# Eight groups of block products in a gated MLP's up projection instead of seven, with three reorderings beside it

## The chip, the cores and the metric

The kernel runs on one core of a Trainium2 chip. The metric is the device time of one execution in microseconds; three executions of the kernel before took 675.86, 676.35 and 676.62 us. The five engines of the core are named PE (TensorE, matrix products; PEld is its loading of weights), DVE (VectorE), ACT (ScalarE), POOL (GpSimd) and SP (SyncE, which issues most of the DMAs). They run side by side; each takes its instructions in the order in which the program issued them, and waits on semaphores where an operand is not ready or a buffer is not free.

## The reference

One decoder layer for a sequence of T = 512 tokens and D = 1024 features, all in float32. Its first part (a conditioned norm, an input projection, two kinds of attention heads, an output projection) is not touched by the change. The second part is:

```python
h2 = rmsnorm(x, norm2_g) * (1.0 + sc2) + sh2          # (512, 1024)
u = causal_dwconv(h2 @ w_up, conv_w, conv_b)          # w_up (1024, 2*2816); 3 taps along the tokens
a, v = jnp.split(u, 2, axis=-1)                       # (512, 2816) each
x = x + gt2 * ((jax.nn.silu(a) * v) @ w_down)         # w_down (2816, 1024)
```

`sc2`, `sh2` and `gt2` come from a small conditioning vector: `mod = silu(c) @ w_ada + b_ada`, cut in six.

## The kernel before, in words

**Products.** A float32 operand is split into a high part, rounded to the type that PE multiplies at full rate, and the low rest. `split` (lines 149 to 151) is an ACT cast for the high part and a DVE subtraction for the low part. `mm3` (lines 153 to 156) then issues three products: high times high, high times low and low times high. 512 or 256 columns stream through PE per product.

**Units and stages.** The 2816 features are 22 blocks of 128. Block j and block j + 11 form unit j, j = 0 to 10 (NU = 11). Each block needs two products with h2, one for a and one for v, so a unit has four. In *Up*, the first phase, a plain **stage** makes one of the four: `up_mm` issues 8 x 3 products of 512 columns into a PSUM bank `u`; `post_taps` takes it through the three convolution taps (`taps`: one ACT activation and two DVE operations, lines 1774 to 1776); `post_gate` applies silu on ACT and, once a and v are there, multiplies them on POOL (`gate`). HEAD lists the blocks that go through stages first, BODY those that go last. NH = 8 is the number of head stages, nst the number of all stages.

**Block products.** The units in XS go through `x_group` instead. There the a products of a unit's two blocks are made as one 2 x 2 block product (two halves of the tokens, two halves of the features, two blocks of weights) by the scheme with seven half products in place of eight. So a group has seven `x_mm` of 12 products with 256 columns (PSUM tile `uf`, with regions X, Y, Z, R) and two full v products (PSUM tile `V`, printed as `u`; 24 products of 512 columns each). The operands are sums: those of h2 are made once (`SX`), those of the weights per group, one group ahead, by `prepare_sums`, `prepare_plain`, `prepare_rest` and `prepare_other` on DVE and ACT: splits `b` (plain), `t12` and `x4` (sums), `c` (plain), `v1` and `v2`. What remains of a group after its last product (the add of Y, the taps of V[1] and of uf[0], and the gates) is put in `held` as three functions and run inside the next group, or in the first stage after the last group.

**The order** of all this is the order of the program text; the engines take it as it stands. In every quarter of a group and in every stage, `beside` advances a tick. At given ticks `weight_sums` issues DMAs that sum blocks of w_down in HBM for the second phase (some on SP, the accumulating ones on POOL), and `put_by` stores the finished products of a unit (`PB`, into `later`) in HBM. XT is the tick of the first stage after the groups; from the second of these stages on, at every other tick, `put_by` splits one of the first EARLY units' other products (`PA`) by `a_split`.

**The last gate, gt2,** is summed beside the groups: `last_add` scales a fetched piece of w_ada on ACT, adds it on POOL into the buffer `gt2`, and fetches the next one on SP; sixteen pieces in all, the first eight for the left half. Each half is then split (`last_split`: `rhi`, `rlo`), summed over the partitions and spread to all of them by two PE products (`last_spread`, line 1527), and copied back on ACT (`last_out`).

**Down,** the second phase, takes 22 blocks u. Blocks 0 to 10 use the `PA` products of units 0 to 10, blocks 11 to 21 the `PB` products. `dn_load` fetches weights on SP three blocks ahead, `dn_split` splits those of the next block (and the unit's `PA`, where it was not split early), `dn_mm` issues the products. PRE = 4 of the `PB` products come back from HBM early: `back` at block u - EARLY + 1 and `a_split` at block u - EARLY, for u counted from EARLY. Line 2124 stores the last `PB` products in block 1; SP waits there for POOL's gates.

Of the kernel before, what the change touches and what calls it, by code (L numbers as in the profile page):

```python
# [50 lines left out]
EPOS = 1  # L51
VLAG = 1
ADL = 1
EARLY = 4
PRE = 4
NU = NFF // 2
XS = (2, 3, 4, 5, 6, 7, 8)
HEAD = (0, 11, 1, 12)
BODY = (9, 20, 10, 21)
PAIRS = tuple(range(NU))  # L60
ADAS = (3, 4, 2)
ADW = 1024
# [47 lines left out]
def hybrid_layer_kernel(ctx: ExitStack, tc: tile.TileContext, d: dict, out: bass.AP, dbg=None):  # L110
# [21 lines left out]
    def PS(s="ps"):  # L132
        return psum.tile([P, 512], F32, tag="b", name=nm(s))

    def TMP(shape, dt=F32, tag="tmp"):
        n = 1
        for a in shape[1:]:
            n *= a
        if n > 256:
            return tp.tile(shape, dt, tag="t2", name=nm(tag), bufs=8)  # L140
        return tp.tile(shape, dt, tag="t1", name=nm(tag), bufs=4)
# [4 lines left out]
    def f32(ap):  # L146
        return ap.bitcast(F32)

    def split(hi, lo, src, eng=None):
        sc.copy(hi, src)  # L150
        (eng or ve).tensor_tensor(lo, src, f32(hi), ALU.subtract)  # L151

    def mm3(o, ah, al, bh, bl, start, stop):
        pe.matmul(o, ah, bh, start=start, stop=False, skip_group_check=True)  # L154
        pe.matmul(o, ah, bl, start=False, stop=False, skip_group_check=True)  # L155
        pe.matmul(o, al, bh, start=False, stop=stop, skip_group_check=True)  # L156
# [45 lines left out]
    def up_load(f):  # L202
        return load(f"up{f}", [2, KT, P], *[((slice(None), h), wu_view[:, :, h * FF + f * P:h * FF + (f + 1) * P])
                                            for h in range(2)])

    def x_load(j, h):
        return load(f"u{'xv'[h]}{j}", [2, KT, P],
                    *[((slice(None), r), wu_view[:, :, h * FF + f * P:h * FF + (f + 1) * P])
                      for r, f in enumerate((j, j + NU))])

    x_loads = [x_load(j, h) for j in XS for h in range(2)]
    loads += [*[up_load(f) for f in HEAD[:-1]], x_loads[0], up_load(HEAD[-1])]
# [3 lines left out]
    last_x = len(loads)  # L216
    loads += [up_load(f) for f in BODY]
    issued = []
# [14 lines left out]
    def take(name):  # L233

        i = taken[0]
        assert loads[i][0] == name, (loads[i][0], name)
        n = max(i + 2, min(i + 3, last_x)) if i >= first_x else i + 2
        while len(issued) < min(n, len(loads)):
            issue()
        taken[0] += 1  # L240
        return issued[i]
# [1252 lines left out]
    def last_fetch(s):  # L1494
        if last_at[0] < 2 * KT:
            q, k = divmod(last_at[0], KT)
            last_at[0] += 1
            r = TMP([P, 512], tag="aw")
            sp.dma_start(r, ada_view[:, k, s * D + q * 512:s * D + q * 512 + 512])
            last_raw.append((r, q, k))  # L1500
# [6 lines left out]
    def last_add(s, res):  # L1507
        r, q, k = last_raw.pop(0)
        acc = res[:, q * 512:(q + 1) * 512]
        sc.activation(r, r, AF.Copy, scale=cs[:, k:k + 1])  # L1510
        gp.tensor_tensor(acc, acc, r, ALU.add)  # L1511
        last_fetch(s)
# [3 lines left out]
    def last_split(res, q):  # L1516
        assert all(raw[1] > q for raw in last_raw)
        hi, lo = (TMP([P, 512], F32R, tag=t) for t in ("rhi", "rlo"))
        split(hi, lo, res[:, q * 512:(q + 1) * 512])
        last_parts.extend((hi, lo))  # L1520
# [8 lines left out]
    def last_out(res, q):  # L1529
        sc.copy(res[:, q * 512:(q + 1) * 512], last_ps.pop())  # L1530
# [227 lines left out]

    NF = HEAD + BODY

# [52 lines left out]
    def put_by(now):  # L1813
        for j in sorted(full_at, key=full_at.get):
            if now >= full_at[j] + 4:
                del full_at[j]
                sp.dma_start(later[j], PB.pop(j)[:, 0:3])
                if place[j] < EARLY:
                    unsplit.append(j)
# [68 lines left out]
    gt2 = wp.tile([P, D], F32, tag="xin", name="gt2", bufs=1)  # L1888
    lo_half, hi_half, full = slice(0, 256), slice(256, 512), slice(0, 512)
    nst = 2 * len(NF)  # L1890
    NH = 2 * len(HEAD)
    XT = NH + 4 * len(XS)
    for i in range(NT):
# [44 lines left out]
    def h_block(r, q):  # L1938
        sl = slice(256 * r, 256 * r + 256)
        return [[h2T[2 * q + k // 2][e][:, k % 2, sl] for k in range(4)] for e in range(2)]  # L1940

    def x_mm(o, w, rhs, start=True):
        for k in range(4):
            mm3(o, w[0][:, k], w[1][:, k], rhs[0][k], rhs[1][k], start and k == 0, k == 3)

    def half(w, b):
        return w[0][:, b], w[1][:, b]
# [6 lines left out]
    def prepare_sums(n):  # L1954
        raw = take(f"ux{XS[n]}")
        b11, b21, b12, b22 = (raw[:, r, k:k + 4] for r in range(2) for k in (0, 4))
        t = G([2, 4, P], s="t12")
        ve.tensor_tensor(t[:, 0], b11, b12, ALU.add)
        ve.tensor_tensor(b12, b12, b22, ALU.add)
        ve.tensor_tensor(t[:, 1], b12, b11, ALU.add)  # L1960
        prep[n] = {"raw": raw, "t": t}
# [14 lines left out]
    def prepare_other(n):  # L1976
        p = prep[n]
        p["other"] = take(f"uv{XS[n]}")
        v, t = ((KT, P), "v1"), ((2, 4, P), "t12")
# [9 lines left out]
    def x_group(n):  # L1989
        j, p = XS[n], prep[n]  # L1990
        more = n + 1 < len(XS)
        ops = {q: [[z[:, k] for k in range(4)] for z in SX[q]] for q in SX}
        h11, h12, h22 = h_block(0, 0), h_block(0, 1), h_block(1, 1)
        uf = PS("uf"), PS("uf")
        X, Y, Z, R = uf[0][:, 256:512], uf[0][:, 0:256], uf[1][:, 0:256], uf[1][:, 256:512]
        V = PS("u"), PS("u")
        m1, n5, u2 = (TMP([P, 256], tag=z) for z in ("m1", "n5", "u2"))
        beside()
        x_mm(X, half(p["b"], 0), h11)
        x_mm(Y, half(p["b"], 1), h12, False)  # L2000
        held.pop(0)()
        split(*p["t12"], p.pop("t"))
        sc.copy(m1, X)
        v_mm(V[0], p["v1"], range(4))
        held.pop(0)()
        last_add(5, gt2)
        beside()
        x_mm(X, half(p["t12"], 1), ops[2], False)
        x_mm(Z, half(p["t12"], 0), ops[1])
        sc.copy(u2, X)  # L2010
        sc.copy(n5, Z)
        v, t = ((KT, P), "v2"), ((4, P), "x4")
        for shape, name in ((v, t) if n % 2 or not more else (t, v)):
            p[name] = room(shape)
        split(*p["v2"], p.pop("other")[:, 1])
        held.pop(0)()
        v_mm(V[0], p["v1"], range(4, KT))
        if more:
            prepare_sums(n + 1)
        beside()  # L2020
        x_mm(X, half(p["c"], 0), ops[3], False)
        x_mm(Z, half(p["c"], 1), ops[4], False)
        taps(V[0], 1, j)
        split(*p["x4"], p.pop("t4"))
        ve.tensor_tensor(Z, Z, u2, ALU.subtract)
        ve.tensor_tensor(R, n5, X, ALU.subtract)  # L2026
        if more:
            prepare_plain(n + 1)
        else:
            last_add(5, gt2)  # L2030
        v_mm(V[1], p["v2"], range(4))
        taps(uf[1], 0, j + NU)
        last_add(5, gt2)
        beside()
        v_mm(V[1], p["v2"], range(4, KT))
        if more:
            prepare_rest(n + 1)
        else:
            last_add(5, gt2)
        x_mm(X, p["x4"], h22, False)  # L2040
        if more:
            prepare_other(n + 1)
        else:
            piece(True)
        del prep[n]

        def first():
            ve.tensor_tensor(Y, Y, m1, ALU.add)
            taps(V[1], 1, j + NU)

        def second():
            gate(0, j + NU)
            taps(uf[0], 0, j)

        def third():
            gate(0, j)
            gate(1, j)
            gate(1, j + NU)

        held.extend((first, second, third))  # L2060
# [30 lines left out]
    for st in range(NH, nst):  # L2091
        beside()
        if st == nst - 3:
            dn_load(0)
        elif st == nst - 1:
            dn_load(1)
        if st in (NH + 2, NH + 4):
            last_spread()
        up_mm(st, full)
        if held:  # L2100
            for f in held:
                f()
            held.clear()
        elif st > NH + 1:
            if st > NH + 2:
                post_gate(st - 3)
            post_taps(st - 2)
        if st in (NH + 1, NH + 3):
            last_split(gt2, st == NH + 3)
        if st in (NH + 2, NH + 4):  # L2110
            last_out(gt2, st == NH + 4)
    dn_split(0)
    post_gate(nst - 3)
    post_taps(nst - 2)
# [14 lines left out]
    for u in range(NU - 1):  # L2129
        ahead_of(u)  # L2130
        if u == 0:
            post_gate(nst - 2)
            post_gate(nst - 1)
        if 0 <= u - EARLY + 1 < PRE:
            back(PAIRS[u - EARLY + 1])
        if 0 <= u - EARLY < PRE:
            a_split(u - EARLY + NU, PB.pop(PAIRS[u - EARLY]))
        for m in TERMS[0]:
# [83 lines left out]
    t = TMP([P, T])[:, 0:256]  # L2222
# [36 lines left out]
```

## Time and profile before

| | |
|---|---|
| median of three executions | 676.35 us (675.86 to 676.62) |
| the profiled execution, whole | 675.84 us |
| its span, first to last instruction | 674.0 us |
| busy share of the span: PE, DVE, ACT, POOL | 98%, 81%, 57%, 26% |
| granted PE clock | 0.998 of full speed |
| first group of block products begins | 368.16 us after the span's start |
| seventh group ends | 516.42 |
| Down begins | 562.26 |

The profile is one execution, recorded by the hardware. Times in it count from the first instruction; between its span and the execution's time lie 1.84 us. A row of a timeline gives the start, the duration, the engine, the line of the kernel, the operation, the tiles written and read (without their numbers), shape and count; in brackets the engine's idle time before it and what ended that. A line can be that of a helper: L150 and L151 are the two halves of every `split`, L154 to L156 the three products of `mm3`, so the tiles tell which one it is. Products overlap in PE, so the distance from one start to the next is what a product costs, not its duration.

### The profile page before, as it was taken

The page shows a single profiled execution, that of the slowest core. Times are in us where ns is not written, and L with a number is a line of the kernel's source. Part 1 is how long each engine was busy: PE and PEld are TensorE (multiplying, and loading weights), DVE is VectorE, ACT ScalarE, POOL GpSimd, SP SyncE. Part 2 cuts the span into 40 slices and gives each one's busy share as a digit, 9 for nine tenths or more (in the row PEclk, how much of TensorE's full clock was granted, in tenths as well). Part 3 has the DMA queues.
Part 4 walks back from the last instruction along what each step waited for, and adds up shares of the span by engine and source line. Part 5 has one row for each costly group of instructions (what it writes and reads, how often), then busy time and mean ns, then how long its engine had stood idle before and what let it go on. Part 6 is the DMA issues. An engine that isn't in the chain of part 4 may idle for free.

```text
span 674.0 us, 11718 instructions
## 1 busy us (share of the span) xinstructions
PE 661.5 (98%) x4400; PEld 558.2 (83%) x4400; DVE 547.5 (81%) x1038; ACT 382.7 (57%) x713; POOL 177.5 (26%) x172
## 2 busy tenths in 40 slices
PE   8999999999999999999999999999999999999996
PEld 4778898788988888888988898898988788888885
DVE  5788988979899879688779678988888758785997
ACT  5755447756687678245555455554655556664451
POOL 1006111000010100100365455666556645000000
PEclk9999999999999999999999999999999999999999
DMA  9936264576122416144748799999997765966662
GB/s 329 411 153 205 95 197 133 183 240 220 44 85 78 143 32 230 55 130 153 233 138 226 228 221 289 242 291 274 265 266 186 219 217 162 361 219 248 219 280 94
DMA packets 101885, 134.67 MB, mean 200 GB/s; under 512 B 6507, under 2 KB 67780, under 8 KB 101829
## 3 DMA queue, kind: packets, MB, share of 16 engines
q1 hardware_dynamic: 96885, 121.28, 53.5%
q0 software_dynamic: 4512, 11.54, 10.1%
q10 hardware_dynamic: 432, 1.12, 0.5%
q8 instruction: 34, 0.56, 0.3%
q14 instruction: 22, 0.18, 0.1%
HBM read 125.39 MB, written 31.60 MB: 233 GB/s over the span
## 4 chain that ended last, share of the span: by engine, by line
PE 82%; DVE 10%; ACT 5%; issue 1%; DMA 1%; ACTq 0%; DVEq 0%
PE u L154 8%; PE u L155 8%; PE u L156 8%; PE dn L154 5%; PE dn L156 5%; PE dn L155 5%; PE uf L156 4%; PE uf L155 3%; PE uf L154 3%; PE accq L680 3%; PE oh L154 2%; PE oh L156 2%; PE oh L155 2%; PE oT L1149 2%; PE F L1120 2%; PE pT L154 2%
## 5 line engine op out<-in xcount | busy, mean ns | idle before, releaser
L151 DVE TENSOR_TENSOR wlo<-raw,whi 128x1024 fp32r<-128x1024 f32 (+1 forms) x52 | 66.3, 1277 | 43.3 <-ACT whi L150 43.2
L154 PE MATMUL u<-h2h,whi 128*128 128x512 f32 (+1 forms) x240 | 90.4, 377 | 0.0
L155 PE MATMUL u<-h2l,whi 128*128 128x512 f32 (+1 forms) x240 | 90.2, 376 | 0.0
L156 PE MATMUL u<-h2h,wlo 128*128 128x512 f32 (+1 forms) x240 | 90.0, 375 | 0.0
L150 ACT CAST whi<-raw 128x1024 fp32r<-128x1024 f32 (+1 forms) x52 | 53.0, 1020 | 32.5 <-PE u L155 25.7
L156 PEld LDWEIGHTS u<-h2h,wlo 128*128 128x128 f32 x240 | 45.2, 188 | 8.3
L154 PEld LDWEIGHTS u<-h2h,whi 128*128 128x128 f32 x240 | 45.3, 189 | 7.5
L155 PEld LDWEIGHTS u<-h2l,whi 128*128 128x128 f32 x240 | 45.3, 189 | 7.4
L150 ACT CAST whi<-wd 128x1024 fp32r<-128x1024 f32 x20 | 21.1, 1055 | 39.8 <-PE dn L156 39.8
L372 POOL TENSOR_TENSOR hrs<-hrs,mhalf 128x4 f32<-128x4 f32 (+2 forms) x16 | 18.6, 1173 | 90.7 <-DVE hrs L371 88.6
L1087 ACT ACTIVATE pt<-pt,mx 128x128 f32<-128x128 f32 (+3 forms) x64 | 35.9, 564 | 9.1 <-DVE mx L1071 8.1
L154 PE MATMUL pT<-hT,whi 128*128 128x512 f32 x96 | 38.3, 399 | 0.0
L151 DVE TENSOR_TENSOR wlo<-wd,whi 128x1024 fp32r<-128x1024 f32 x20 | 24.9, 1247 | 16.1 <-ACT whi L150 16.1
L156 PE MATMUL pT<-hT,wlo 128*128 128x512 f32 x96 | 37.5, 391 | 0.0
L155 PE MATMUL pT<-hT,whi 128*128 128x512 f32 x96 | 37.5, 391 | 0.0
L155 PE MATMUL dn<-wlo,as 128*128 128x512 f32 x88 | 34.4, 390 | 0.1
L154 PE MATMUL dn<-whi,as 128*128 128x512 f32 x88 | 34.3, 389 | 0.0
L156 PE MATMUL dn<-whi,as 128*128 128x512 f32 x88 | 34.2, 389 | 0.0
L1511 POOL TENSOR_TENSOR gt<-gt,aw 128x512 f32<-128x512 f32 x16 | 23.0, 1441 | 41.1 <-ACT aw L1510 41.0
L1127 ACT COPY pT<-F 128x512 f32<-128x512 f32 (+2 forms) x52 | 25.8, 499 | 13.2 <-PE F L1120 13.2
L1071 DVE CUSTOM_DVE_ANT_0 pt<-S,cmask 128x128 f32<-128x128 f32 (+3 forms) x64 | 29.7, 485 | 2.2 <-PE S L1067 2.0
L1774 ACT ACTIVATE y<-uf,cv 128x512 f32<-128x512 f32 x14 | 10.9, 776 | 30.2 <-DVE uf L2026 28.2
(409 smaller groups left out, 2040.7 us busy)
## 6 DMA issues: line engine op xcount, KB each, us to landing
raw<-in_w_up SPq DMA_DIRECT2D x44, 512.0 KB, 6.3
aw<-in_w_ada SPq DMA_DIRECT2D x24, 512.0 KB, 4.0
ada<-in_ada_first SPq DMA_DIRECT2D x16, 512.0 KB, 8.0
raw<-in_w_in SPq DMA_DIRECT2D x7, 1024.0 KB, 4.9
wt<-in_w_down POOLq DMA_DIRECT2D x11, 512.0 KB, 8.1
wd<-in_w_down SPq DMA_DIRECT2D x11, 512.0 KB, 5.1
wt<-in_w_down SPq DMA_DIRECT2D x10, 512.0 KB, 6.2
wt<-in_w_down POOLq DMA_DIRECT2D x5, 1024.0 KB, 10.0
```

The costliest lines, as they stand in the source:

```text
L150: sc.copy(hi, src)
L151: (eng or ve).tensor_tensor(lo, src, f32(hi), ALU.subtract)
L154: pe.matmul(o, ah, bh, start=start, stop=False, skip_group_check=True)
L155: pe.matmul(o, ah, bl, start=False, stop=False, skip_group_check=True)
L156: pe.matmul(o, al, bh, start=False, stop=stop, skip_group_check=True)
L372: gp.tensor_tensor(o, o, mhalf[:, 0:n], ALU.pow)
L680: pe.matmul(accq[i], h[:, e, i * P:(i + 1) * P], w[:, f], start=(k + e + f == 0), stop=(e == 1 and k == KT - 1), skip_group_check=True)
L1071: ve.tensor_tensor_reduce(pt[:, e * W:(e + 1) * W], ps[:, e * W:(e + 1) * W], cmask[:, 512 - W:512], -1.0, 1e30, ALU.add, ALU.min, mx[:, e ...
L1087: sc.activation(pt[:, sl], pt[:, sl], AF.Exp, bias=mx[:, e:e + 1], scale=-1.0, accum_out=su[:, h % 2, e:e + 1])
L1120: pe.transpose(ps[:, j * P:(j + 1) * P], src[:, j * P:(j + 1) * P], ident)
L1127: sc.copy(pT, ps[:, 0:n * P])
L1511: gp.tensor_tensor(acc, acc, r, ALU.add)
```

## The change

Unit 9 moves from BODY into XS: eight groups instead of seven, four last stages instead of eight. In a group, the split of t12 stands ahead of the first held function instead of behind it. Since the sixteen `last_add` now fit two to a group, the last group has no extra ones; at the place of the second extra one stands the split of the gate's left half, so its spread comes in the first stage after the groups (NH), the right half's split in stage NH + 1 and its spread in stage NH + 3. EARLY is 2 instead of 4: two early splits of `PA`, at two of the four remaining ticks after XT, and read-backs of `PB` two blocks earlier in Down.

```diff
-EARLY = 4
+EARLY = 2
 PRE = 4
 NU = NFF // 2
-XS = (2, 3, 4, 5, 6, 7, 8)
+XS = (2, 3, 4, 5, 6, 7, 8, 9)
 HEAD = (0, 11, 1, 12)
-BODY = (9, 20, 10, 21)
+BODY = (10, 21)
@@ x_group
         x_mm(X, half(p["b"], 0), h11)
         x_mm(Y, half(p["b"], 1), h12, False)
+        split(*p["t12"], p.pop("t"))
         held.pop(0)()
-        split(*p["t12"], p.pop("t"))
         sc.copy(m1, X)
...
         if more:
             prepare_plain(n + 1)
-        else:
-            last_add(5, gt2)
         v_mm(V[1], p["v2"], range(4))
         taps(uf[1], 0, j + NU)
         last_add(5, gt2)
...
         if more:
             prepare_rest(n + 1)
         else:
-            last_add(5, gt2)
+            last_split(gt2, 0)
@@ stages after the groups
-        if st in (NH + 2, NH + 4):
+        if st in (NH, NH + 3):
             last_spread()
         up_mm(st, full)
...
-        if st in (NH + 1, NH + 3):
-            last_split(gt2, st == NH + 3)
-        if st in (NH + 2, NH + 4):
-            last_out(gt2, st == NH + 4)
+        if st == NH + 1:
+            last_split(gt2, 1)
+        if st in (NH, NH + 3):
+            last_out(gt2, st == NH + 3)
```

## The prediction

> **What bounds the kernel now.** I read the page first, then one table of windows cut at the boundaries of the Up groups, then the timelines of single engines where that table shows lost time.
>
> ```profile
> span 674.0 us, 11718 instructions
> PE 661.5 (98%) x4400; PEld 558.2 (83%) x4400; DVE 547.5 (81%) x1038; ACT 382.7 (57%) x713; POOL 177.5 (26%) x172
> 368.16:389.17 21.01, 21.01 (x134) 19.07 (x132) 14.54 (x19) 10.83 (x16) 11.83 (x11) 1.00 0.76 226
> 389.17:410.19 21.02, 21.02 (x135) 19.08 (x133) 16.96 (x20) 10.77 (x17) 11.67 (x12) 1.00 1.03 275
> 410.19:431.44 21.25, 21.25 (x135) 19.13 (x134) 18.11 (x22) 11.55 (x18) 12.87 (x12) 1.00 1.03 268
> 431.44:452.67 21.23, 21.23 (x135) 19.13 (x133) 18.09 (x22) 11.54 (x18) 12.83 (x12) 1.00 1.01 263
> 452.67:473.92 21.25, 21.25 (x135) 19.14 (x134) 18.10 (x22) 11.53 (x18) 12.89 (x12) 1.00 1.03 266
> 473.92:495.16 21.24, 21.24 (x134) 19.13 (x133) 18.09 (x22) 11.52 (x18) 12.86 (x12) 1.00 0.95 241
> 495.16:516.42 21.26, 21.26 (x135) 19.14 (x134) 15.57 (x19) 12.74 (x20) 13.75 (x14) 1.00 0.96 268
> 516.42:527.32 10.90, 10.90 (x50) 9.02 (x49) 9.13 (x10) 4.63 (x8) 5.72 (x5) 1.00 0.79 204
> 527.32:529.08 1.76, 0.74 (x4) 0.30 (x2) 1.76 (x2) 1.70 (x2) 1.68 (x2) 1.00 0.33 99
> 529.08:540.02 10.94, 10.94 (x50) 9.01 (x49) 7.11 (x8) 4.32 (x7) 6.05 (x7) 1.00 0.81 200
> 540.02:540.48 0.46, 0.46 (x4) 0.38 (x3) 0.00 (x0) 0.46 (x1) 0.38 (x2) 1.00 0.51 89
> 540.48:562.26 21.78, 21.78 (x98) 18.02 (x96) 15.89 (x17) 11.59 (x16) 9.51 (x9) 1.00 0.70 216
> ```
>
> In a window row stand the length, then busy time of PE, PEld, DVE, ACT and POOL, the granted clock, and the DMA share. PE issues without a break, at clock 1.00. The time of this part is therefore the count of products times their spacing, plus the few waits of PE itself. Seven rows are the seven groups of block products, the next five the single stages (two, a spread of the gate, two, a spread, four). The two first groups take 21.01 and 21.02 us, the five others 21.23 to 21.26: some 0.23 us is lost in each. The first spread takes 1.76 us where the second takes 0.46. Both losses are PE waits for a VectorE split:
>
> ```profile
> 415.93 0.28 PE L155 MATMUL uf<-sx,whi 128*128 128x256 f32 x1
> 416.19 0.39 PE L156 MATMUL uf<-sx,wlo 128*128 128x256 f32 x1
> 528.74 0.50 PE L1527 MATMUL ps<-rlo,onesr 128*128 128x512 f32 x1 [1.02 <-DVE rlo L151]
> ```
>
> In the first two rows the product with the low part of t12 starts 0.26 us after its neighbour instead of 0.12; the last row is the first spread's second product, with PE's idle time of 1.02 us and its releaser.
>
> **The change part by part.**
>
> *An eighth group for four stages (XS, BODY).* Unit 9 leaves the single stages. Four stages are 96 wide products: 21.78 us (last row of the table). A group is 84 products of 256 columns and 48 of 512: 21.02 us without waits. PE saves 0.76 us, and nothing hides PE. Weights come as ux9 and uv9, four transfers of 512 KB, in place of up9 and up20, also four; the tick counter advances four either way, so the weight sums on SP and POOL keep their ticks.
>
> *t12 split ahead of the taps.* The VectorE order at the start of the last group, and ScalarE's:
>
> ```profile
> 496.98 1.22 DVE L151 TENSOR_TENSOR wlo<-raw,whi 128x1024 fp32r<-128x1024 f32 x1
> 498.11 0.42 DVE L2048 TENSOR_TENSOR uf<-uf,m 128x256 f32<-128x256 f32 x1
> 498.45 0.74 DVE L1775 SCALAR_TENSOR_TENSOR y<-u,cv,y 128x511 f32<-128x511 f32 x1
> 499.22 0.75 DVE L1776 SCALAR_TENSOR_TENSOR y<-u,cv,y 128x510 f32<-128x510 f32 x1
> 499.88 1.22 DVE L151 TENSOR_TENSOR wlo<-t,whi 128x1024 fp32r<-128x1024 f32 x1
> 495.46 0.78 ACT L1774 ACTIVATE y<-u,cv 128x512 f32<-128x512 f32 x1
> 496.13 1.04 ACT L150 CAST whi<-t 128x1024 fp32r<-128x1024 f32 x1
> ```
>
> The split ends at 501.10, where PE, at the group's start plus 5.63 plus 0.24, wants it at 501.03; signalling makes the rest. Moved up, it starts when v1's split ends, 498.11, its cast, now ahead of the activation, being done by 495.46 + 1.04 = 496.5. It ends at 499.3, 1.7 us early. What is queued behind it is late by 1.2 us: the add of Y, the two taps of V[1], and ScalarE's activation of the next taps, which waits for Y. They free PSUM banks of the former group, which PE wants again only in the next group, and VectorE idles afterwards (15.57 to 18.11 busy of 21.2 us). Next late would be v1's own split, which nothing here moves. Saved: the excess of five groups over 21.02, 0.23+0.21+0.23+0.22+0.24 = 1.13 us.
>
> *The gate's first split in the last group, spread at NH, second split at NH+1, spread at NH+3.* The rows at the last group's end:
>
> ```profile
> 512.19 1.32 ACT L1510 ACTIVATE aw<-aw,cs 128x512 f32<-128x512 f32 x2
> 513.12 0.75 DVE L1776 SCALAR_TENSOR_TENSOR y<-uf,cv,y 128x510 f32<-128x510 f32 x1
> 514.50 2.04 DVE L151 TENSOR_TENSOR wg<-raw,wg 128x1024 fp32r<-128x1024 f32 x1 [0.63 <-DMA wt<-wt]
> 516.46 2.31 DVE L151 TENSOR_TENSOR wlo<-raw,whi 128x1024 fp32r<-128x1024 f32 x1
> 526.91 1.77 DVE L151 TENSOR_TENSOR rlo<-gt,rhi 128x512 fp32r<-128x512 f32 x1
> 538.28 0.68 DVE L151 TENSOR_TENSOR rlo<-gt,rhi 128x512 fp32r<-128x512 f32 x1
> ```
>
> One of ScalarE's two scalings (0.66 each) goes, with its POOL add and fetch, spread over eight groups instead; the cast of rhi takes its place. On VectorE rlo follows the taps that end at 513.87 and takes 0.68 to 1.77 us, so it is there by 515.6 at the latest; PE reaches it at 516.4. The first stage's split then starts at 514.6 to 515.6 and takes 1.22 to 2.04: done 515.8 to 517.6, wanted (group's end without the wait 516.18, spread 0.46, two wide products 0.46) at 517.1. I take no wait, since the removed POOL add was one of those that ran beside it; the bound is 0.5 us. The second split keeps its place behind the stage-9 split, and its spread now comes a stage, 5.4 us, later. Saved: 1.76 - 0.46 = 1.30 us.
>
> *Half as many stages after the groups.* VectorE must do in 22.70 us (21.78 and two spreads of 0.46): Y 0.42, five pairs of taps at 1.49, seven splits of 1024 at 1.22 (three of stage weights, two early, two of the first Down block), rlo 0.68: 17.1. Cover is 5.6 us. The end of the part is as before: the last taps wait for the split that waits for the last stage, and PE loses some 0.3 us in the first Down block (row 562.26 below, 5.71 against 5.44); unchanged. Down's first load is nearer to its use:
>
> ```profile
> 532.46 1.31 POOL L1753 DMA_DIRECT2D wt<-in_w_down  x1
> 541.43 0.48 SPq L1755 DMA_DIRECT2D wt<-wt  x1
> 541.95 0.59 SPq L1848 DMA_DIRECT2D raw<-wt  x1
> 556.79 1.06 ACT L150 CAST whi<-raw 128x1024 fp32r<-128x1024 f32 x1
> ```
>
> On SP it stands behind a weight sum that waits for POOL's accumulate, 9.0 us after that is issued (532.46 to 541.43), and its cast comes 5.5 us ahead of Down. The accumulate keeps its tick, 39, which is now the end of the last group, behind the last gate add: at 534 to 536 (estimate, the former last group's scalings at 512.19 to 513.5 plus the 20.1 us by which the last group moves, and an add). So the load goes out at 543.5 to 545.5 and, by the longest landing quoted below, 7.8, is there by 553.3; the cast wants it at 559.0 - 5.5 = 553.5. I cost it at nothing.
>
> *EARLY 2 for 4.* Two splits of PA (1.2 us of VectorE each) leave the single stages for Down, u = 1 and 2, and the four read-backs of PB move from u = 3..6 to 1..4, their splits from 4..7 to 2..5.
>
> ```profile
> 562.26:567.97 5.71, 5.62 (x25) 4.40 (x24) 4.88 (x6) 5.05 (x6) 0.94 (x2) 1.00 0.68 262
> 584.29:589.73 5.44, 5.44 (x26) 4.51 (x25) 4.37 (x5) 3.74 (x5) 0.00 (x0) 1.00 1.04 417
> 560.47 12.60 SPq L1817 DMA_DIRECT2D later<-gb  x2
> 574.86 1.21 DVE L151 TENSOR_TENSOR as<-ga,as 128x1024 fp32r<-128x1024 f32 x1
> 585.24 0.95 DVE L151 TENSOR_TENSOR as<-gb,as 128x768 fp32r<-128x768 f32 x1
> DMA to landing us min/median/max: 4.1/5.9/7.8
> ```
>
> (The last row is that of the read-backs, line 1837.) SP stands from 560.47 to 573.07 before the last store of PB, and the first read-back now comes right behind it: issued 573.1, landed 577.2 to 580.9. VectorE meets its split in order, with the split for u = 4 behind it: a cast of at most 1.04 (the row of the 1024 form above), 0.95, then 1.21 for PA and 1.21 for the first half of the weights, which PE needs at 584.29: landing plus 4.4. That is 581.6 to 585.3: cost 0 to 1.0, taken 0, by the median landing (583.4). From there on VectorE has 0.95 + 3 x 1.21 = 4.6 us of work in a block of 5.44.
>
> *Sum.* Before, from the first group to Down: 148.26 + 45.84 = 194.10. After: 8 x 21.02 + 21.78 + 2 x 0.46 = 190.86. Saved 3.24 (0.76 + 1.13 + 1.30, and 0.05 of rounding). The profiled execution took 675.84 us; 672.60 after. It lay 0.51 under the median of 676.35, so 673.1 for the median.
>
> [...] Wide products stand 21.78/96 = 0.227 us apart in this trace, narrow ones (21.02 - 48 x 0.227)/84 = 0.120. [...]
>
> **The rivals.**
>
> 1. *The waits move instead of going* (contention stretches v1's or the gate's split again, as the 2.04 to 2.31 us rows beside 1.22 show). Then only the eighth group pays: 673.1 + 6 x 0.23 + 1.30 = 675.8; half of it 674.5. Against it: 1.7 and 0.8 us of room. 12%.
> 2. *VectorE bounds the shortened stages.* If all seven splits took 2.31 and rlo 1.77, VectorE would need 17.1 + 7 x 1.09 + 1.09 = 25.8 of 22.70 us: 673.1 + 3.1 = 676.2. It decides from 5.6 us of stretching; the first four stages and their spread, with such rows in them, held 9.13 + 1.76 + 7.11 = 18.0 of 23.6. 5%. [...]
> 3. *The read-back in Down, on the slower side.* A PB buffer or its transfer one block (5.44) later than the median landing lands 11.3 us after issue, where 6.8 is free (584.29 - 4.4 - 573.1), and costs 4.5: 677.6, slower. It decides from a landing of 6.8 + 3.24 = 10.0 us; the longest here took 7.8. 7%.
> 4. *Narrow products not worth it*: a spacing of (21.78 - 48 x 0.227)/84 = 0.130 us would cancel the 0.76: 673.9. The seven groups show 0.120. 3%.
>
> **How the numbers follow.** The forecast, 673.1, holds 73%, alone 672.3 to 674.0 (its lower end without the first Down block's 0.3 and with 0.5 as between profile and median; its upper end with the bounds of 0.5 and half of 1.0). 0.2% of 676.35 is 1.35 us, about what a measurement of this kernel tells from none: faster is below 675.0. Faster 0.73 + 0.03 + half of rival 1 = 0.82; same, the rest of rival 1 and most of rival 2 and some of 3, 0.12; slower 0.06. The range 672.1 to 675.2 takes in rival 4 and half of rival 1.
>
> **What would show it.** Eight rows of group windows at 21.0; no PE start held by wlo in them; both spreads near 0.46; Down begins at 559.0 after the span's start (562.26 now), and lasts as long as before. Wrong: a group row at 21.2, a spread above 1 us, a Down block over 5.5 beside the first, or PE in the single stages waiting for wlo.

## The result, and the profile after

| | before | after |
|---|---|---|
| median, six executions each | 676.44 us (675.80 to 678.68) | 672.74 us (672.38 to 673.51) |
| ratio | | 0.9946 [0.9933, 0.9959] |
| the profiled execution, whole / its span | 675.84 / 674.0 | 672.67 / 670.9 |
| first group begins / Down begins | 368.16 / 562.26 | 368.29 / 559.16 |
| from the one to the other | 194.10 | 190.87 |

The change saves 3.7 us of the median. The forecast of 673.1 is a ratio of 0.9952 and lies inside the interval; from the first group to Down the trace saves 3.23 us, where 3.24 was worked out.

The page of the kernel after:

```profile
span 670.9 us, 11810 instructions
PE 659.4 (98%) x4436; PEld 559.1 (83%) x4436; DVE 554.9 (83%) x1047; ACT 385.9 (58%) x718; POOL 177.6 (26%) x172
```

Its windows, cut at the same places as before: the first, third and last group (in the five left out the length is 21.02), a spread, three stages, a spread, the fourth stage, and the first and the fifth block of Down. The columns are those of the prediction's first fence.

```profile
368.29:389.30 21.01, 21.01 (x133) 19.07 (x132) 14.92 (x19) 11.19 (x16) 12.09 (x11) 1.00 0.79 226
...
410.32:431.34 21.02, 21.02 (x134) 19.08 (x133) 18.13 (x22) 11.67 (x18) 12.50 (x12) 1.00 1.01 252
...
515.42:536.44 21.02, 21.02 (x134) 19.08 (x133) 16.14 (x21) 12.15 (x19) 11.65 (x12) 1.00 0.76 179
536.44:536.90 0.46, 0.46 (x4) 0.38 (x3) 0.46 (x1) 0.46 (x2) 0.00 (x0) 1.00 0.60 76
536.90:553.24 16.34, 16.34 (x74) 13.52 (x73) 12.44 (x13) 8.39 (x12) 8.66 (x8) 1.00 0.86 305
553.24:553.70 0.46, 0.46 (x4) 0.38 (x3) 0.21 (x1) 0.21 (x1) 0.00 (x0) 1.00 1.14 272
553.70:559.16 5.46, 5.46 (x26) 4.50 (x24) 4.98 (x5) 3.19 (x5) 3.92 (x3) 1.00 0.92 239
559.16:564.87 5.71, 5.62 (x25) 4.40 (x24) 5.54 (x7) 5.71 (x7) 0.82 (x2) 1.00 0.15 58
...
581.19:586.63 5.44, 5.44 (x26) 4.51 (x25) 5.44 (x6) 5.44 (x7) 0.00 (x0) 1.00 1.04 412
```

Every group now takes 21.01 or 21.02 us, both spreads 0.46. The lengths tell it, not PE's busy time, which hid waits of 0.23 us before (21.25 of 21.25): eight times 21.02, 0.46 twice, and 16.34 + 5.46 for 96 products at 0.227. PE waits for nothing in Up any more. The 0.3 us in Down's first block (5.71 against 5.44) is left, as foretold.

The VectorE splits that PE waited for before, in VectorE's timeline of the kernel after, last group (t12, then the gate and the first stage weights):

```profile
517.26 1.22 DVE L151 TENSOR_TENSOR wlo<-raw,whi 128x1024 fp32r<-128x1024 f32 x1
518.39 1.22 DVE L151 TENSOR_TENSOR wlo<-t,whi 128x1024 fp32r<-128x1024 f32 x1
533.78 1.05 DVE L151 TENSOR_TENSOR rlo<-gt,rhi 128x512 fp32r<-128x512 f32 x1
534.76 1.21 DVE L151 TENSOR_TENSOR wg<-raw,wg 128x1024 fp32r<-128x1024 f32 x1
536.07 1.23 DVE L151 TENSOR_TENSOR wlo<-raw,whi 128x1024 fp32r<-128x1024 f32 x1
```

The split of t12 follows v1's directly and ends at 519.61; PE wants it at 515.42 + 5.87 = 521.29 (5.63 + 0.24 after the group's start, as in the prediction). The two weight splits, 2.04 and 2.31 us before, take 1.21 and 1.23.

Two further waits of PE, which the comparison of starts shows in both kernels: 0.25 us in Down's first block, 0.30 in its last. PE's timeline of the kernel after:

```profile
563.69 0.39 PE L156 MATMUL dn<-wg,as 128*128 128x512 f32 x1
564.17 0.47 PE L154 MATMUL dn<-wg,as 128*128 128x512 f32 x1
...
656.74 0.39 PE L154 MATMUL dn<-whi,as 128*128 128x512 f32 x1
657.26 0.50 PE L155 MATMUL dn<-wlo,as 128*128 128x512 f32 x1
```

Steps of 0.48 and 0.52 us stand where 0.227 is usual. The step behind such a wait is longer too, by 0.08 to 0.11 us; where an amount "after it" is counted below, it is this.

### The profile page after: what moved, and what is told of

It reads as the page before. It is cut to its first block, busy times and chain, and to the rows that moved or that the text cites. A ratio compares the mean times of both kernels' runs of the same rounds, so it can differ in the third digit from the quotient of the medians.

```text
span 670.9 us, 11810 instructions
## 1 busy us (share of the span) xinstructions
PE 659.4 (98%) x4436; PEld 559.1 (83%) x4436; DVE 554.9 (83%) x1047; ACT 385.9 (58%) x718; POOL 177.6 (26%) x172
## 4 chain that ended last, share of the span: by engine, by line
PE 82%; DVE 10%; ACT 5%; issue 1%; DMA 1%; ACTq 0%; DVEq 0%
PE u L154 8%; PE u L155 8%; PE u L156 8%; PE dn L154 5%; PE dn L155 5%; PE dn L156 5%; PE uf L156 4%; PE uf L155 4%; PE uf L154 4%; PE accq L680 3%; PE oh L154 2%; PE oh L155 2%; PE oh L156 2%; PE oT L1149 2%; PE F L1120 2%; PE pT L154 2%
## 5 line engine op out<-in xcount | busy, mean ns | idle before, releaser
L151 DVE TENSOR_TENSOR wlo<-raw,whi 128x1024 fp32r<-128x1024 f32 (+1 forms) x50 | 62.6, 1254 | 35.8 <-ACT whi L150 35.6
L154 PE MATMUL u<-h2h,whi 128*128 128x512 f32 (+1 forms) x224 | 84.2, 376 | 0.0
L155 PE MATMUL u<-h2l,whi 128*128 128x512 f32 (+1 forms) x224 | 84.1, 375 | 0.0
L156 PE MATMUL u<-h2h,wlo 128*128 128x512 f32 (+1 forms) x224 | 83.7, 374 | 0.0
L150 ACT CAST whi<-raw 128x1024 fp32r<-128x1024 f32 (+1 forms) x50 | 50.8, 1018 | 20.7 <-PE u L155 14.2
L156 PEld LDWEIGHTS u<-h2h,wlo 128*128 128x128 f32 x224 | 42.2, 188 | 7.7
L154 PEld LDWEIGHTS u<-h2h,whi 128*128 128x128 f32 x224 | 42.3, 189 | 6.8
L155 PEld LDWEIGHTS u<-h2l,whi 128*128 128x128 f32 x224 | 42.3, 189 | 6.5
L1511 POOL TENSOR_TENSOR gt<-gt,aw 128x512 f32<-128x512 f32 x16 | 20.7, 1296 | 50.5 <-ACT aw L1510 50.5
L1774 ACT ACTIVATE y<-uf,cv 128x512 f32<-128x512 f32 x16 | 12.5, 780 | 37.2 <-DVE uf L2026 33.4
```

## The experiments

Eleven kernels in three batches, each on one chip beside the kernel before. The medians of before were 676.06, 675.84 and 676.10. "Up" in this table is the time from the first group's first product to Down's first product, "Down" from there to the start of PE's last product, both in PE's timeline of one profiled execution (before 194.10 and 105.44, after 190.87 and 105.40).

| kernel | median, us | ratio to before | Up | Down |
|---|---|---|---|---|
| e1, t12 alone | 674.93 | 0.9984 [0.9970, 0.9999] | 192.94 | 105.44 |
| e2, gate alone | 674.71 | 0.9975 [0.9960, 0.9990] | 192.72 | 105.44 |
| e3, group alone | 673.81 | 0.9959 [0.9944, 0.9974] | 192.25 | 105.41 |
| e4, after, Down's waits | 671.40 | 0.9928 [0.9903, 0.9953] | 190.86 | 104.64 |
| e5, after, EARLY 3 | 672.78 | 0.9961 [0.9948, 0.9974] | 190.87 | 105.45 |
| e6, after, read-backs late | 676.47 | 1.0006 [0.9997, 1.0014] | 190.87 | 107.77 |
| e7, after, one more on VectorE | 674.34 | 0.9982 [0.9972, 0.9992] | 190.86 | 106.99 |
| e8, after, two more | 679.78 | 1.0058 [1.0046, 1.0070] | 190.86 | 112.41 |
| e9, before, gate sums earlier | 676.10 | 1.0003 [0.9992, 1.0013] | 193.86 | 105.45 |
| e10, e7 with taps first | 672.15 | 0.9947 [0.9933, 0.9960] | 191.31 | 105.10 |
| e11, nine groups on e4 | 675.29 | 0.9990 [0.9978, 1.0002] | 190.12 | 108.70 |

A whole time carries one thing more than these two columns: in the profiled executions of e6, e10 and e11 the first group began at 369.8 to 369.9, in the others at 368.0 to 368.5, with the difference there by the 500th product (94.2, against 92.3 to 92.8). So a median is read here to about a microsecond, and the two columns to 0.1.

### e1: the split of t12 alone

```diff
 # kernel before
+        split(*p["t12"], p.pop("t"))
         held.pop(0)()
-        split(*p["t12"], p.pop("t"))
```

> The kernel before with one edit: the split of t12 stands ahead of the first held function. Theory (three separate terms that add up): all seven groups at 21.0 us, Down begins 1.1 us earlier than before (561.1 after the span's start instead of 562.26), time 1.1 below that of before, ratio 0.9983. Rival (the waits move): PE waits in another place of the group, most likely for v1's split, rows stay near 21.2 and the time within 0.3 us of before.

Up is 1.16 us shorter. A window of e1, the third group:

```profile
410.17:431.19 21.02, 21.02 (x134) 19.08 (x133) 18.10 (x22) 11.66 (x18) 12.49 (x12) 1.00 1.03 261
```

The third group, 21.25 before, is at 21.02 with nothing else changed. The first spread still waits: its two products stand 1.42 us apart. The step of 1.13 us is the order of these two lines.

### e2: the gate's early split alone

```diff
 # kernel before: seven groups, eight stages
         else:
             last_add(5, gt2)
+            last_split(gt2, 0)
@@ stages after the groups
-        if st in (NH + 2, NH + 4):
+        if st in (NH, NH + 3):
             last_spread()
...
-        if st in (NH + 1, NH + 3):
-            last_split(gt2, st == NH + 3)
-        if st in (NH + 2, NH + 4):
-            last_out(gt2, st == NH + 4)
+        if st == NH + 1:
+            last_split(gt2, 1)
+        if st in (NH, NH + 3):
+            last_out(gt2, st == NH + 3)
```

> The kernel before with one edit: seven groups and eight stages, both extra scalings kept in the last group and behind the second of them the split of the gate's left half; its spread in stage NH, the right half's split in NH + 1 and spread in NH + 3. Theory: the first spread takes 0.46 us instead of 1.76, Down begins 1.3 us earlier (561.0), ratio 0.9981. Because the extra scaling is still there, ScalarE's cast for the first stage is 0.6 us later than in the changed kernel: a wait of at most 0.5 us in the first stage is possible. Rival (VectorE bounds the end of the groups): the first stage loses what the spread gains, 1 us or more, and the time stays within 0.3 us of before.

Up is 1.38 us shorter, 1.30 of it at the first spread, which takes 0.46 us. VectorE's timeline of e2 around the group's end:

```profile
514.37 0.69 DVE L151 TENSOR_TENSOR rlo<-gt,rhi 128x512 fp32r<-128x512 f32 x1 [0.20 <-ACT rhi L150]
515.32 1.99 DVE L151 TENSOR_TENSOR wg<-raw,wg 128x1024 fp32r<-128x1024 f32 x1 [0.25 <-ACT wg L150]
517.23 2.31 DVE L151 TENSOR_TENSOR wlo<-raw,whi 128x1024 fp32r<-128x1024 f32 x1
```

The extra sums are still there, and so are the slow splits of 1.99 and 2.31 us; rlo is now ahead of them, and PE, which starts the spread at 516.73, finds it done at 515.06. So the early split is enough.

### e3: the eighth group alone

The kernel after, with t12 and the gate's order as before. The gate's two splits come in the second and third stage after the groups (NH+1, NH+2), each spread one stage behind its split.

```diff
 # kernel after
-        split(*p["t12"], p.pop("t"))
         held.pop(0)()
+        split(*p["t12"], p.pop("t"))
...
-        else:
-            last_split(gt2, 0)
...
-        if st in (NH, NH + 3):
+        if st in (NH + 2, NH + 3):
             last_spread()
...
-        if st == NH + 1:
-            last_split(gt2, 1)
-        if st in (NH, NH + 3):
+        if st in (NH + 2, NH + 3):
             last_out(gt2, st == NH + 3)
+        if st in (NH + 1, NH + 2):
+            last_split(gt2, st == NH + 2)
```

> The changed kernel with two of its parts undone: t12 split behind the first held function again, and the gate's left half split in stage NH + 1 and spread in NH + 2 (right half: split NH + 2, spread NH + 3, since there are only four stages). Theory: the eighth group alone pays 0.76, and the t12 wait comes in six groups instead of five (-0.23), so 0.5 us below before if the first spread waits 1.3 as before; the second spread, a stage after its split, may wait up to 0.7 more: time between 0.2 above and 0.5 below that of before, ratio 0.9992 to 1.0003. Rival (narrow products or the shorter run of stages cost something of their own): slower than before by over 0.5 us. Rival (the group is worth more than its products say): more than 1 us below.

This missed: the gain of 0.41% is far outside the expected 0.9992 to 1.0003. The groups from the third on are at 21.24 again, as expected, but the first spread doesn't wait. PE's timeline of e3 at that spread, and then VectorE's ahead of it:

```profile
548.87 0.39 PE L1527 MATMUL ps<-rhi,onesr 128*128 128x512 f32 x1
549.09 0.39 PE L1527 MATMUL ps<-rlo,onesr 128*128 128x512 f32 x1
```

```profile
535.40 1.48 DVE L151 TENSOR_TENSOR wg<-raw,wg 128x1024 fp32r<-128x1024 f32 x1
537.62 1.22 DVE L151 TENSOR_TENSOR wlo<-raw,whi 128x1024 fp32r<-128x1024 f32 x1 [0.74 <-ACT whi L150]
...
546.99 1.77 DVE L151 TENSOR_TENSOR rlo<-gt,rhi 128x512 fp32r<-128x512 f32 x1
```

The split of the gate is as slow as before (1.77), yet it starts 1.88 us ahead of the spread, where it started 0.41 ahead in the kernel before (526.91 and 527.32). The two splits at the group's end take 1.48 and 1.22 us in place of 2.04 and 2.31. What is gone is most of POOL's work beside them. POOL's timeline, kernel before and then e3:

```profile
512.79 2.66 POOL L1511 TENSOR_TENSOR gt<-gt,aw 128x512 f32<-128x512 f32 x2
...
516.00 1.69 POOL L1511 TENSOR_TENSOR gt<-gt,aw 128x512 f32<-128x512 f32 x1
```

```profile
534.50 1.29 POOL L1511 TENSOR_TENSOR gt<-gt,aw 128x512 f32<-128x512 f32 x1 [0.15 <-ACT aw L1510]
```

Before, POOL's second and third sum of the gate run beside the two splits until 517.69; in e3 the only one there ends at 535.79. The first of the two splits also starts some 0.65 us later in the kernel before, counted from the group's end, as its cast stands behind a second scaling on ScalarE; by these times that alone would not have held up the next split, whose cast comes later still, but no run takes the two apart. In eight groups the sixteen sums fit without extras in the last, so the eighth group takes this wait away too: 0.76 + 1.30 - 0.23 (one more group with t12's wait) = 1.83, against 1.85 measured. The reading of these rows is that POOL's sums stretch the splits beside them: 1.22 us without a sum, 2.04 and 2.31 with one.

### e9: the gate's extra sums in the first two groups

It tests that reading on the kernel before, without an eighth group and without an early split.

```diff
 # kernel before
         if more:
             prepare_plain(n + 1)
-        else:
+        if n < 2:
             last_add(5, gt2)
...
         if more:
             prepare_rest(n + 1)
-        else:
-            last_add(5, gt2)
```

> The kernel before with the two extra scalings of the gate taken out of the last group and put into the first two; splits and spreads of the gate stay where they were. Question: what made the first spread wait? Theory A (the extra scalings: their POOL additions stretch the VectorE splits at the groups' end to 2.04 and 2.31 us, and the delay is still there when the gate's split comes): those splits take 1.2 to 1.5 us, the first spread 0.46 instead of 1.76, Down begins 1.3 us earlier, ratio 0.9981. Theory B (the place of the split in the second stage, as in the prediction): the spread still takes 1.5 us or more, time as before.

On the spread the reading holds. VectorE's timeline of e9 at the end of the last group and in the second stage, and PE's at the spread:

```profile
517.29 1.23 DVE L151 TENSOR_TENSOR wlo<-raw,whi 128x1024 fp32r<-128x1024 f32 x1 [0.74 <-ACT whi L150]
...
526.66 1.77 DVE L151 TENSOR_TENSOR rlo<-gt,rhi 128x512 fp32r<-128x512 f32 x1
```

```profile
528.53 0.39 PE L1527 MATMUL ps<-rhi,onesr 128*128 128x512 f32 x1
528.76 0.39 PE L1527 MATMUL ps<-rlo,onesr 128*128 128x512 f32 x1
```

The missing wait alone would prove little, since PE itself reaches this spread 1.1 us later in e9, counted from the first group, and the gate's split ends only 0.25 us earlier on the clock (528.43 against 528.68). But the work ahead of that split hangs on PE: the cast of the last weights starts 1.46, 1.42 and 1.42 us ahead of the last group's end in the kernel before, e9 and e3. Counted from that end (516.42, 517.63, 537.96), the gate's split is done after 12.26 us before, and after 10.80 in both e9 and e3, where PE wants it at 11.13.

On the time it failed: no gain. The price moved with the sums. PE's timeline of e9 in the third group:

```profile
413.41 0.40 PE L155 MATMUL u<-h2l,whi 128*128 128x512 f32 x1
414.49 0.50 PE L156 MATMUL u<-h2h,wlo 128*128 128x512 f32 x1 [0.68 <-DVE wlo L151]
```

A step of 1.08 us where 0.227 is usual: the wait for v1's split, with 0.11 after it, gives back 0.96 of the 1.30, and t12's wait behind it is 0.35 in place of 0.23. Up is 0.24 shorter in the end. This wait comes by another way than the one that it replaces: the second group's last scaling on ScalarE starts 2.04 us later than in the kernel before (410.02 for 407.98), after 1.80 us of waiting for its fetched piece of w_ada, and the casts for the third group stand behind it. Where the sums fall decides, not that there are sums.

### e4: Down's two waits

```diff
 # kernel after
     dn_load(2)
-    dn_split(1)
     post_taps(nst - 1)
+    dn_split(1)
@@ the last block's first weights take a "wg" buffer in place of "whi"
-        wsp[u] = dn_part(r1) + dn_part(r0)
+        wsp[u] = dn_part(r1, u == 2 * NU - 1) + dn_part(r0)
```

> The changed kernel with the two PE waits that it still has taken away: the taps of the last stage stand ahead of the split for the second Down block, and the last Down block's first weights are split into another buffer than the one that the block before last still reads. Theory: what PE does not wait for is what the kernel gains: the first Down block takes 5.44 us instead of 5.71, the wait of 0.41 near the end goes too, 0.7 us below the changed kernel (672.0, ratio to before 0.9935). Rival: the second Down block's split, now 1.5 us later, makes PE wait there instead (block 2 over 5.5), and nothing is gained at the end, because the last chain of outputs on VectorE sets it.

A window of e4, the first block of Down:

```profile
558.83:564.27 5.44, 5.44 (x25) 4.50 (x24) 5.29 (x6) 5.24 (x7) 1.98 (x3) 1.00 0.17 69
```

The first block is at 5.44, and Down as a whole is 0.76 us shorter than in after. The six executions, 671.02 to 672.16, lie below all six of after (672.38 to 673.51), though the two were not measured beside each other. This is the fastest version found.

### e5 and e6: the early splits and the read-backs

```diff
 # e5, kernel after
-EARLY = 2
+EARLY = 3
-            if unsplit and XT < now and (now - XT) % 2:
+            if unsplit and XT < now:
 # e6, kernel after
-        if 0 <= u - EARLY + 1 < PRE:
-            back(PAIRS[u - EARLY + 1])
+        if 0 <= u - EARLY < PRE:
+            back(PAIRS[u - EARLY])
```

> The changed kernel with EARLY 3 and an early split at every tick after XT: three early splits of PA in the four stages, read-backs of PB one Down block later. Theory (both are covered by PE): time as the changed kernel within 0.3 us (672.4 to 673.1), no wait of PE in stages or Down beyond the 0.3 of the first Down block. Rival (VectorE is close to bounding the stages): its 1.2 us more there shows as a PE wait of 0.5 to 1.2 us in the last stages or the first Down block.

> The changed kernel with each of the four early read-backs issued in the block that splits it, instead of one block earlier; on SP the first then stands behind the three loads for block 5. Theory (rival 3 of the prediction, made to happen): issue near 574.0, landing 577.3 to 581.4, VectorE holds the split for block 4 behind it, ready 4.4 us after the landing, 581.7 to 585.8, and PE wants it at 581.19: PE waits 0.5 to 4.6 us at block 4, some of it again at block 5, Down is longer by 1 to 5 us in all. Other theory (the order on VectorE does not bind, room is larger than I reckoned): no wait, time within 0.3 us of the changed kernel.

e5 changes nothing: Up and Down as in after. In e6 each read-back goes out a block later. PE's timeline of e6 at the fifth block:

```profile
582.62 0.39 PE L156 MATMUL dn<-wg,as 128*128 128x512 f32 x1
583.84 0.50 PE L154 MATMUL dn<-whi,as 128*128 128x512 f32 x1 [0.82 <-ACT whi L150]
585.29 0.50 PE L155 MATMUL dn<-wlo,as 128*128 128x512 f32 x1 [0.95 <-DVE wlo L151]
```

Steps of 1.21 and 1.45: with the 0.11 after them 2.3 us too many, and Down is 2.37 longer. The read-back that stands in front of those splits is the one that the prediction named. Another 1.56 us of the profiled execution lies in the late first group; whether the other executions of e6 have it too isn't shown.

### e7, e8 and e10: how much cover VectorE has

One (e7) or two (e8) additions of 1024 columns per stage whose results are not used, 4.9 and 9.8 us in four stages. e10 is e7 with the last taps in front of dn_split(1), as in e4.

```diff
 # kernel after, in each stage after the groups; e8 with range(2)
+        for _ in range(1):
+            spare = G([2, T], s="spare")
+            ve.tensor_tensor(spare, f32(h2T[0][0]), f32(h2T[0][0]), ALU.add)
```

> The changed kernel with one more VectorE operation of 1024 columns per stage after the groups, four in all, results unused: 4 x 1.2 = 4.9 us of VectorE in 22.7. In the changed kernel VectorE is busy 0.46 + 12.44 + 0.21 + 4.98 = 18.1 of these, so 4.6 us are free. Theory (cover as counted): PE waits at most 0.5 us more than now. Rival (the order of the work, not its sum, binds: each stage's split or taps come late at once): PE waits 1.2 us or more.

> As the one before with two extra VectorE operations per stage, eight in all: 9.8 us against 4.6 us free. Theory: VectorE becomes the bound, 18.1 + 9.8 - 22.7 = 5.2 us are over; Down has 0.8 to 1.5 us of room per block in its first blocks, so that PE loses 3 to 5.2 us in the last stages and the first Down blocks: 675.7 to 677.9. Rival (VectorE work can be put off into Down, where it has room): a loss under 1.5 us.

> The changed kernel with one extra VectorE operation per stage (four, 4.9 us, results unused) as tried before, and the last stage's taps ahead of the split for the second Down block. The extra operations alone cost PE 1.80 us at its wait for the last taps, against 0.33 without them. Theory (the order binds, not the sum: the taps stand behind two splits that nobody wants yet): the wait goes, no PE wait over 0.3 us in the first two Down blocks, time as the changed kernel within 0.4 us. Rival (the sum binds: VectorE has run out of cover): the loss of 1.5 us stays, in the second block instead of the first.

PE's timeline of e7 in Down's first block, VectorE's of e7, and VectorE's of e10 at the same place:

```profile
563.72 0.39 PE L156 MATMUL dn<-wg,as 128*128 128x512 f32 x1
565.74 0.47 PE L154 MATMUL dn<-wg,as 128*128 128x512 f32 x1 [1.64 <-DVE y L1776]
```

```profile
562.93 1.22 DVE L151 TENSOR_TENSOR wg<-raw,wg 128x1024 fp32r<-128x1024 f32 x1
...
564.85 0.75 DVE L1776 SCALAR_TENSOR_TENSOR y<-u,cv,y 128x510 f32<-128x510 f32 x1
```

```profile
564.63 0.75 DVE L1776 SCALAR_TENSOR_TENSOR y<-u,cv,y 128x510 f32<-128x510 f32 x1
565.29 1.21 DVE L151 TENSOR_TENSOR wlo<-raw,whi 128x1024 fp32r<-128x1024 f32 x1
```

In e7 PE waits 2.02 - 0.48 = 1.54 us longer than in after, for the last taps, which stand behind the two splits of the next block's weights (the second one is shown). In e10 Down begins at 561.23, and the same taps end 4.15 us behind that, in place of 6.42 behind 559.18; PE has no wait there, Down is 0.3 shorter than in after, and the extra work costs nothing. (The 0.44 us by which Up is longer in that execution is a wait in a group, ahead of all extra work.) So the cover was short by the order of the instructions, not by VectorE's time: e7's rival and e10's theory came true.

In e8 the splits themselves are late. PE's timeline of e8 where Down begins, and the window behind the wait:

```profile
564.36 0.79 PE L155 MATMUL dn<-wlo,as 128*128 128x512 f32 x1 [4.68 <-DVE wlo L151]
564.95 0.63 PE L156 MATMUL dn<-whi,as 128*128 128x512 f32 x1
565.38 0.63 PE L154 MATMUL dn<-whi,as 128*128 128x512 f32 x1
```

```profile
564.36:567.45 3.09, 3.09 (x8) 2.47 (x9) 3.05 (x4) 0.00 (x0) 0.53 (x1) 0.52 0.55 217
```

The wait of 4.84 us beyond the usual step comes first; a further one of 0.83 for the taps stands at 570.21. Between them seven products at a granted clock of 0.52 take 3.09 us (the row's x8 takes in a neighbour), most of them 0.427 from start to start, and with that 1.5 us more than at the usual spacing, which no theory had. Down is 7.0 us longer for 9.8 of work, and the median of 679.78 lies above the 675.7 to 677.9 that were expected.

### e11: a ninth group, no stages at all

On e4: unit 10 in XS, BODY empty. The gate's two splits and spreads, the two early splits of PA and Down's first three loads and first split go into the last group; what it holds back runs at Down's start.

> Nine groups and no stage after them, on top of the kernel without the two Down waits: unit 10 goes through a group too; in the last group, where nothing is prepared for a next one, stand both splits and spreads of the gate, two splits of PA, the first three Down loads and the first Down split. Theory: the ninth group saves 0.76 again, 670.7 (ratio 0.9917), if Down's first products find their banks and operands; VectorE must do the held work (3.4 us) and the second Down block's split (2.4) in the first Down block of 5.44. Rival (there is no stage left to hide the last group's rest): PE waits 1 to 4 us at the start of Down, and the kernel is slower than with eight groups: 672 to 675.

Up is 0.74 shorter than in e4, the price of a group once more, but Down is 4.1 longer. PE's timeline of e11 at Down's start and in its second block:

```profile
561.73 0.50 PE L155 MATMUL dn<-wg,as 128*128 128x512 f32 x1 [1.39 <-DVE wg L151]
...
567.73 0.50 PE L154 MATMUL dn<-whi,as 128*128 128x512 f32 x1 [0.48 <-ACT whi L150]
569.38 0.50 PE L155 MATMUL dn<-wlo,as 128*128 128x512 f32 x1 [1.15 <-DVE wlo L151]
```

Waits of 1.55, 0.65 and 1.43 beyond the usual steps, with 0.11 after two of them 3.85. The two splits for the first Down block end at 562.80, behind the taps and a split of PA in VectorE's queue, and the second block's cast stands behind the held work on ScalarE: without stages nothing hides what a group leaves behind. The rival came true, with the median 0.3 us above its range. Nine groups in another order of the last one were not tried.

## Why the prediction was right

*The eighth group, 0.76 us.* Right. The eighth row of windows is 21.02 us, the single stages cost 0.227 a product as before, and e11's ninth group brings 0.74 once more. Rival 4 (narrow products at 0.130) is answered by the same row: 21.02 stands there, not 21.78.

*t12, 1.13 us.* Right, and shown by e1 alone (1.16). The end of the split was put 1.7 us ahead of its use; it is 521.29 - 519.61 = 1.68. Nothing behind it became late. The room beside it is thin, though: rival 1 counted 1.7 and 0.8 us, but v1's split, which the edit doesn't move, ends only 0.30 to 0.33 us ahead of its use from the third group on, before and after. In the one profile of e10, which has the same order, PE waits 0.44 us for it in the fifth group.

*The gate, 1.30 us.* The size and the early split's effect are right: e2 has them alone. Incomplete was the account of why. The prediction put the whole saving on the earlier place of the split and used the removed POOL sum only as a reason for no new wait. e3 shows that with eight groups the wait is gone at the old place too, since those sums had stretched the two splits ahead of it (2.04 and 2.31 to 1.48 and 1.22). The three terms are not separate gains: 1.16, 1.38 and 1.85 make 4.39, for 3.23 together. So in the changed kernel the early split seems to buy room only: the split ends 0.33 us ahead of its use in e3 (548.76 to 549.09), and 1.8 in after (534.83 to 536.67). The changed kernel with nothing but the early split undone was not run. The step of the first-stage split, bounded at 0.5 and taken as none, held.

*Down's first load.* Free, as costed, but with more room than was reckoned. SP's timeline of the kernel after:

```profile
539.93 0.38 SPq L1848 DMA_DIRECT2D raw<-wt  x1
```

It goes out at 539.93, not at 543.5 to 545.5: the wait of 9.0 us in front of the weight sum was taken over from one row of before, and here it is 4.5 (POOL issued its accumulate at 534.23).

*EARLY, 0 of 0 to 1.0.* Right by the number, with two errors that cancel. The last store of PB lets go of SP 12.5 us after Down's start, not 10.8. It waits for POOL's last gates, of which the last two operations take 1.60 us each where they took 0.74: VectorE splits beside them without a pause, where before it had one of 1.58 us. (The two splits of PA that came down fill it; with one of them fewer, in e5, SP is let go at 12.5 all the same.) The read-back then lands in less than the median it was taken at. SP's timeline, and ScalarE's and VectorE's, which show the landing and the split that PE needs at 581.19:

```profile
555.94 15.75 SPq L1817 DMA_DIRECT2D later<-gb  x2
571.82 0.36 SPq L1837 DMA_DIRECT2D gb<-later  x1
```

```profile
575.17 0.84 ACT L150 CAST as<-gb 128x768 fp32r<-128x768 f32 x1 [5.31 <-DMA gb<-later]
```

```profile
578.18 1.22 DVE L151 TENSOR_TENSOR wlo<-wd,whi 128x1024 fp32r<-128x1024 f32 x1
```

Landed by 575.17, 3.35 us after issue where 5.9 was taken; the split ends at 579.40, 1.8 us early. e6 shows the wait that rival 3 named, at the place it named: a cast that starts 4.3 us later than this, counted from Down's start, costs 2.3, and 4.3 less 1.8 is 2.5.

*The cover of 5.6 us on VectorE.* Here a step failed, though the time didn't hang on it. It was a sum over the stages, 22.70 less 17.1; the rows of after leave 4.6, as VectorE is busy 0.46 + 12.44 + 0.21 + 4.98 there. e7 puts in 4.9 and loses 1.54, since the last taps stand in line behind two splits; rival 2 decides from less than 4.9 us of stretching, not from 5.6. e10 shows that the order does it.

*Against the median.* The trace saves 3.2 us, the medians 3.7; the interval of the ratio is 1.8 us wide, and the remaining half microsecond is inside it. The likeliest value of 673.1 was 0.36 too high.

## What to carry to other kernels

When one engine issues without a break, a table of windows cut at equal pieces of work finds waits of 0.2 us that a page doesn't show, and each can be costed before anything is built. Several edits that help the same wait don't add: ask of each whether the wait would still be there with the others done. An engine's free time in a stage is no cover for what stands last in its queue (e7: 4.6 us free, 4.9 put in, 1.54 lost, and nothing lost in e10's order); look at what the next stage's first instruction waits for and at what is issued ahead of that.

## What the runs showed of the hardware

*The granted clock after a wait.* In e8, 4.7 us without a product left the next ones 0.427 us apart in place of 0.227, with a granted clock of 0.52 for 3.1 us; behind that, from 567.45 to 570.21, the clock is 1.00 and the products are 0.23 apart again. Waits of 1.64 us (e7) and 1.39 (e11) left the spacing as it was, so far as the starts of the products show. What a wait between 1.64 and 4.7 us does to the products behind it is not shown. At the end of the profiles, where no product follows, the clock is still 1.00 in 671.00 to 671.50 of before, 3.8 us behind the start of PE's last product (667.70), and in 667.00 to 669.00 of after, 4.4 us behind it (664.56); it is 0.50 in 672.00 to 673.00 and in 670.00 to 670.50.

*The type of the splits.* Their products of 512 columns stand 0.227 us apart; four bf16 products of 512 columns in the trace of before (line 528, from 14.94 on) stand 0.21 to 0.22 apart. The "full rate" in the kernel's description is shown here no further than this.

*Sums on GpSimd and splits on VectorE took longer side by side.* A split of 1024 columns took 1.22 us alone and up to 2.31 beside a POOL sum of 512 columns; the POOL sum, 1.29 at its shortest in these rows, took 1.69 there. In e9, with the extra sums moved away, the split of 2.31 took 1.23, and the gate's split behind it was done 10.80 us after the group's end in place of 12.26.

*The start varies.* Identical instructions reached the first group at 368.0 to 368.5 us in ten of the profiled executions and at 369.8 to 369.9 in three. What sets it is not shown.
